# First gate pair: eight loaded operands are split ahead of the first product, four others one step sooner

## The chip, the cores and the metric

The kernel runs on one core of a Trainium2 chip. The metric is the time of one execution on the device in microseconds (us), the median of several runs. Beside it stands one execution taken by the hardware profiler. Its span, from the first instruction to the last, is what the profile divides up; the execution's own time is a little longer. The engines are named PE (matrix products; PEld is its weight load), ACT (ScalarE), DVE (VectorE), POOL (GpSimd) and SP, which here only issues transfers.

## What is computed

One layer of a hybrid encoder over 1024 prompt frames and 32 sample frames (together 1056 columns), model width 1024. The part that matters here is the merge of the two mixers:

```python
h = rms_norm(x, g_mix)
z = h @ w_in                          # q, k, v, conv_h, conv_B, conv_C, gate_a, gate_b
a = attn_core(q, k, v) @ w_attn_out
bo = (cb * conv) @ w_conv_out
x = x + (sigmoid(ga) * a + sigmoid(gb) * bo) @ w_mix_out
```

Ahead of it stand the norm, the input projection and the windowed attention; behind it a cross-attention into 256 memory tokens, a squared-ReLU MLP of width 4096 and a last norm. `ga` and `gb` are two column blocks of `z`, each 1056 columns of frames by 1024 features.

## The kernel before, in words

**Layout and products.** Features lie on the 128 partitions, frames along the columns, in three chunks of 384, 384 and 288 columns (`CH`). Every float32 operand of a product is split into a rounded part `hi` and a remainder `lo`: ACT copies `hi`, DVE subtracts to get `lo`. A product then takes three matmuls per 128 x 128 block: `wh*hi`, `wh*lo`, `wl*hi`. `gemm` (L195) does this over eight blocks, `product` (L875) over the four blocks of half a weight tile.

**Weights.** They stream in tiles of 128 x 1024 (512 KB). `fetch_w` (L147) issues the load on SP into one of two `wr` buffers, or, during the gate pairs, every third one into a further buffer in the pool `gtop`. `issue_w` (L164) splits the oldest loaded tile (L129 on ACT, L130 on DVE) into one of three `wh` and three `wl` buffers. A `wh` buffer is taken again only when the last product that reads it is done.

**The gate pairs.** For each feature block f from 1 to 7, `gate_pair` (L924) computes gate a and gate b of the first two chunks together, with seven half products in place of eight. Weights `w1` (gate a), `w4`, `w3` (sums of gate weights, made beforehand by POOL in `sum_step`, L718) and `w2` (gate b) are used in that order. The operands come in seven kinds, four blocks each: `b11`, `b21`, `t2` and `n1` are split already and lie in `X` tiles; `n3` and `b22` go into `Y` tiles of the middle chunk and `n4` into `N` tiles. These last three kinds were written to memory as plain float32 (`xs_d`) while the attention output was computed, and have to be loaded again and split. In the order of the code a pair is:

- `A = w1 x b11` (L956), copy `s1 <- A` (L958), then one weight split
- `A += w1 x b21` (L962), its sigmoid (L931) and its multiply by the attention output (L935)
- the gate of the 288-column tail with `w1` (`gate_c2`, L966), where it wasn't made earlier: in the pairs 1, 5, 6 and 7
- one weight split, `B = w4 x t2` (L973), `u2 = B - s1` (L976)
- `C = w3 x n1` (L981), `v = C + s1` (L983), `B += w3 x n3` (L984), `B - v` and its sigmoid
- `C += w4 x b22` (L990), `C - u2` (L992) and its multiply by the attention output
- one weight split, `B += w2 x n4` (L997), `B - s1` (L999) and its sigmoid
- one weight split, the tail's gate with `w2` (L1004)

Three times in a pair `sum_step` is called: POOL sends off a load, does four additions of 128 x 256 (L735) on the tile loaded before, and stores it.

**Loading and splitting operands.** `pump(n)` (L807) does two things: it splits everything that the call before has loaded (L810 on ACT, L811 on DVE), and it issues the next n loads of the list `wanted` (L815 on SP). `open_gates` (L884) puts 20 loads on that list: four of `n3`, four of `b22`, four of `n4` and eight of the convolution branch (`bc_d`). It calls `pump(8)` at once, so that `n3` and `b22` are on their way when the first pair begins. The tiles that the first twelve are loaded into are `Gb0` and `Gb1`, five slots each, two of each kind going to `Gb0` and two to `Gb1`. In the first pair `pump(4)` stands behind the sigmoid and multiply of A (L964): it splits the eight and loads the four of `n4`; `pump(0)` at L988, behind product `n3`, splits those four. In the other pairs there are one load at L964 and one at L979.

**What sets the order.** The code gives the order in which instructions are traced. A planner, which runs when the program is built, puts each engine's instructions in an order of its own by a simulated time; within that order each engine then works strictly one after the other, and waits by semaphores. `pin` (L97) holds an instruction behind the one traced just before it on its engine. The splits of `pump` are pinned in this way; its loads are not, and neither are weight splits, the copy to `s1`, or the matmuls.

Of the kernel before, what the change touches and what calls it, by code (L numbers as in the profile page):

```python
# [40 lines left out]
def hybrid_step(ctx: ExitStack, tc: tile.TileContext, io):  # L41
# [5 lines left out]
    def nm(s):  # L47
        uid[0] += 1
        return f"{s}_{uid[0]}"
# [47 lines left out]
    def pin(ins):  # L97
        return tc.keep_in_program_order(ins)

    def acc_tile(shape):  # L100
        return ps.tile(shape, F32, tag="acc", bufs=n_acc, name=nm("acc"))
# [3 lines left out]
    def tmp(n, dt=F32):  # L105
        return tp.tile([P, n], dt, tag="ct", bufs=NCT, name=nm("ct"))
# [40 lines left out]
    def fetch_w(raw=None):  # L147
        if raw is not None:
            pass
        elif third:  # L150
            third["n"] += 1
        if raw is not None:
            pass
        elif third and third["n"] % 3 == 0:
            raw = third["pool"].tile([P, 4, 256], F32, tag="ws", name=nm("wr3")).rearrange("p q c -> p (q c)")
        else:
            raw = wp.tile([P, 1024], F32, tag="wr", bufs=2, name=nm("wr"))
        src = weight(worder[wpos[0] + len(fetched)])
        load = sp.dma_start(raw.rearrange("p (i c) -> p i c", i=4) if len(src.shape) == 3 else raw, src)
        if third and third["n"] == 3 and third["pool"] is W["pool"]:  # L160
            pin(load)
        fetched.append(raw)

    def issue_w(pieces=(slice(0, 1024),)):  # L164
        if not fetched:
            fetch_w()
        raw = fetched.pop(0)
        key = worder[wpos[0]]
        hi = wp.tile([P, 1024], F32R, tag="wh", name=nm("wh"))
        lo = wp.tile([P, 1024], F32R, tag="wl", name=nm("wl"))  # L170
        if kept.get(key) is not None:
            sp.dma_start(lo.bitcast(F32), kept[key])
            act.copy(hi, raw)
        else:
            for at in pieces:
                split(hi[:, at], lo[:, at], raw[:, at])
            if key in kept:
                kept[key] = dram.tile([P, 1024], F32, name=nm("wl_d"))
                sp.dma_start(kept[key], lo.bitcast(F32))
        ready.append((worder[wpos[0]], (hi, lo)))  # L180
        wpos[0] += 1
# [487 lines left out]
    def gate_slot(c, f):  # L669
        n = CH[c][1]  # L670
        return slot(ga_pool, f"Ga{c}", n, F32) if f < 3 else slot(G["pool"], f"Gb{c}", n, F32)
# [46 lines left out]
    def sum_step():  # L718
        old = W.pop("new", None)
        if pieces:  # L720
            at = pieces.pop(0)
            t = sum_tile(len(pieces))
            if at[0] in ("g", "u"):
                kind, f, q = at
                for e in range(2):
                    src = io["w_in"][34 + 8 * e + f] if kind == "g" else io["w_up"][UP[f][e]]
                    src = src.rearrange("p (h c) -> p h c", h=2)
                    pin(pool_e.dma_start(t[:, 2 * e : 2 * e + 2], src[:, :, 256 * q : 256 * q + 256]))
            else:
                pin(pool_e.dma_start(t, io["w_down"][at]))  # L730
            W["new"] = at, t
        if old:
            at, t = old
            for to, x, y in ((3, 2, 3), (2, 0, 2), (0, 0, 3), (1, 1, 0)):
                pin(pool_e.tensor_tensor(t[:, to], t[:, x], t[:, y], op=ALU.add))  # L735
            if at[0] in ("g", "u"):
                kind, f, q = at
                for w in range(2):
                    pin(pool_e.dma_start((gsum_d[f - 1] if kind == "g" else usum_d[f])[:, w, :, 256 * q : 256 * q + 256], t[:, 2 * w : 2 * w + 2]))
            else:  # L740
                pin(pool_e.dma_start(wsum_d[at], t))
# [65 lines left out]
    def pump(n):  # L807
        for into, at, t, get in coming:
            hi, lo = into[at] = (get(), get())
            pin(act.copy(hi, t))  # L810
            pin(dve.tensor_sub(lo, t, hi.bitcast(F32)))  # L811
        coming.clear()
        for into, at, src, cols, get in wanted[:n]:
            t = cols() if callable(cols) else tmp(cols)
            sp.dma_start(t, src)  # L815
            coming.append((into, at, t, get))
        del wanted[:n]
# [57 lines left out]
    def product(acc, w, half, acts, start):  # L875

        wh, wl = w
        for k, (hi, lo) in enumerate(acts):
            a = slice(512 * half + k * P, 512 * half + k * P + P)
            pe.matmul(acc, wh[:, a], hi, start=(start and k == 0), stop=False, skip_group_check=True)  # L880
            pe.matmul(acc, wh[:, a], lo, start=False, stop=False, skip_group_check=True)  # L881
            pe.matmul(acc, wl[:, a], hi, start=False, stop=(k == 3), skip_group_check=True)  # L882
# [22 lines left out]
    def gate_c2(w):  # L905
        n = CH[2][1]
        a = ps.tile([P, n], F32, tag="pt", bufs=2, name=nm("pa"))
        gemm(a, w, xg[2])
        return a
# [14 lines left out]
    def gate_pair(f):  # L924
        def take(key):
            k, w = ready.pop(0)
            assert k == key, (k, key)
            return w

        def into(t, x):  # L930
            act.activation(t, x, AF.Sigmoid)  # L931
            return t

        def attended(c, t):
            dve.tensor_mul(t, t, la[c])  # L935
            sp.dma_start(m1_d[c][:, f], t)

        la = {}

        def load_a(c):  # L940
            if (c, f) in sa:
                return
            la[c] = tmp(CH[c][1])
            sp.dma_start(la[c], a_d[c][:, f])

        op = lambda kind: [gop[kind, k] for k in range(4)]
        w1 = take(("w_in", 34 + f))
        if f == 1:
            third.update(n=2, pool=Y["top"])
            fetch_w()  # L950
        if f == NF - 1:
            third.clear()
        load_a(0)
        load_a(2)
        A, B, C = (acc_tile([P, 384]) for _ in range(3))
        product(A, w1, 0, op("b11"), True)  # L956
        s1 = Y["top"].tile([P, 384], F32, tag="s1", name=nm("s1"))
        act.copy(s1, A)  # L958
        issue_w()
        if f < NF - 1:  # L960
            fetch_w()
        product(A, w1, 1, op("b21"), False)  # L962
        attended(0, into(tmp(384), A))
        pump(4 if f == 1 else 1)  # L964
        if (2, f) not in sa:
            a2 = gate_c2(w1)  # L966
            t = tmp(CH[2][1])
            dve.tensor_mul(t, a2, R[2])
            attended(2, into(t, t))
        issue_w()  # L970
        fetch_w()
        w4 = take(("g_sum", f - 1, 0))
        product(B, w4, 0, op("t2"), True)  # L973
        load_a(1)
        u2 = Y["top"].tile([P, 384], F32, tag="u2", name=nm("u2"))
        dve.tensor_sub(u2, B, s1)  # L976
        sum_step()
        if f > 1:
            pump(1)  # L979
        w3 = take(("g_sum", f - 1, 1))  # L980
        product(C, w3, 1, op("n1"), True)  # L981
        v = Y["top"].tile([P, 384], F32, tag="v", name=nm("v"))
        dve.tensor_add(v, C, s1)  # L983
        product(B, w3, 0, op("n3"), False)  # L984
        g22 = gate_slot(1, f)
        dve.tensor_sub(g22, B, v)
        sg[1][f] = into(g22, g22)
        pump(0)  # L988
        sum_step()
        product(C, w4, 1, op("b22"), False)  # L990
        t = tmp(384)
        dve.tensor_sub(t, C, u2)  # L992
        attended(1, into(t, t))
        issue_w()
        fetch_w()
        w2 = take(("w_in", 42 + f))
        product(B, w2, 1, op("n4"), False)  # L997
        g21 = gate_slot(0, f)
        dve.tensor_sub(g21, B, s1)  # L999
        sg[0][f] = into(g21, g21)  # L1000
        sum_step()
        issue_w()
        fetch_w()
        a2 = gate_c2(w2)  # L1004
        g2 = gate_slot(2, f)
        dve.tensor_mul(g2, a2, R[2])
        sg[2][f] = into(g2, g2)
# [18 lines left out]
    for f in PAIRS:  # L1026
        worder.extend([("w_in", 34 + f), ("g_sum", f - 1, 0), ("g_sum", f - 1, 1), ("w_in", 42 + f)])
        item(lambda f=f: gate_pair(f))
# [992 lines left out]
```

## Time and profile before

| | before |
|---|---|
| runs, median (lowest to highest) | 1748.65 us (1747.12 to 1750.77), 3 runs |
| profiled execution, its own time | 1748.9 us |
| its span | 1746.4 us |
| granted TensorE clock | 0.998 of full speed |
| DMA | 346.60 MB, mean 198 GB/s |
| the seven gate pairs | about 657 to 800 us of the span |

How to read the lines that follow further down. In the page's first part an engine's busy time stands with its share of the span and its number of instructions. A row of the timeline has start, duration, engine, line of the code, operation, output<-inputs, the number of merged instructions, and in brackets the idle time before it with what released it. Numbers at the end of tile names are left out, so that `acc` stands for the accumulators A, B and C alike, `pa` for the tail's gate, `s` for s1, `u` for u2, and `wr` for a raw weight tile wherever it lies. A row of waits has who waited for whom, total, count and longest. A row of stretches has the stretch, its length, then the busy time of PE, PEld, DVE, ACT and POOL with their counts, the granted clock, the share of DMA and GB/s. Rows of SP are marked SPq.

### The profile page before, as it was taken

The page shows a single profiled execution, that of the slowest core. Times are in us where ns is not written, and L with a number is a line of the kernel's source. Part 1 is how long each engine was busy: PE and PEld are TensorE (multiplying, and loading weights), DVE is VectorE, ACT ScalarE, POOL GpSimd, SP SyncE. Part 2 cuts the span into 40 slices and gives each one's busy share as a digit, 9 for nine tenths or more (in the row PEclk, how much of TensorE's full clock was granted, in tenths as well). Part 3 has the DMA queues.
Part 4 walks back from the last instruction along what each step waited for, and adds up shares of the span by engine and source line. Part 5 has one row for each costly group of instructions (what it writes and reads, how often), then busy time and mean ns, then how long its engine had stood idle before and what let it go on. Part 6 is the DMA issues. An engine that isn't in the chain of part 4 may idle for free. (4 is left out here: it accounts for less than half of the span.)

```text
span 1746.4 us, 32603 instructions
## 1 busy us (share of the span) xinstructions
PE 1725.4 (99%) x12262; PEld 1708.0 (98%) x12262; DVE 1192.7 (68%) x2276; ACT 852.7 (49%) x1660; POOL 593.6 (34%) x667
## 2 busy tenths in 40 slices
PE   9999999999999999999999999999999999999998
PEld 8999999999999999999999999999999999999998
DVE  7776776867676656545677888787666686545675
ACT  8653533535335324434556666765444453333444
POOL 0026366453643444452225232005555410000121
PEclk9999999999999999999999999999999999999999
DMA  4333344333436888877766667775767695555555
GB/s 185 99 129 125 119 133 145 121 134 134 156 127 209 288 294 274 281 231 232 270 222 199 217 225 242 234 258 191 222 223 222 217 321 187 189 192 171 191 170 160
DMA packets 179854, 346.60 MB, mean 198 GB/s; under 512 B 18657, under 2 KB 101249, under 8 KB 179569
## 3 DMA queue, kind: packets, MB, share of 16 engines
q1 hardware_dynamic: 163504, 290.07, 50.5%
q0 software_dynamic: 15568, 53.68, 8.8%
q8 instruction: 96, 1.57, 0.4%
q10 hardware_dynamic: 624, 0.77, 0.1%
q14 instruction: 62, 0.50, 0.1%
HBM read 250.73 MB, written 93.14 MB: 197 GB/s over the span
## 5 line engine op out<-in xcount | busy, mean ns | idle before, releaser
L129 ACT CAST wh<-wr 128x1024 fp32r<-128x1024 f32 (+1 forms) x214 | 223.8, 1046 | 369.3 <-PE acc L1808 124.7
L130 DVE TENSOR_TENSOR wl<-wr,wh 128x1024 fp32r<-128x1024 f32 (+1 forms) x214 | 276.4, 1292 | 126.9 <-ACT wh L129 126.2
L200 PE MATMUL acc<-X,wh 128*128 128x384 f32 (+1 forms) x864 | 281.5, 326 | 0.0
L201 PE MATMUL acc<-X,wh 128*128 128x384 f32 (+1 forms) x864 | 278.6, 322 | 0.2 <-DVE X L280 0.2
L202 PE MATMUL acc<-X,wl 128*128 128x384 f32 (+1 forms) x864 | 277.8, 322 | 0.0
L276 POOL TENSOR_TENSOR xacc<-xacc,ct 128x384 f32<-128x384 f32 (+1 forms) x56 | 76.6, 1370 | 379.5 <-ACT ct L274 377.8
L201 PEld LDWEIGHTS acc<-X,wh 128*128 128x128 f32 x864 | 162.7, 188 | 1.5 <-DVE X L280 0.5
L200 PEld LDWEIGHTS acc<-X,wh 128*128 128x128 f32 x864 | 162.4, 188 | 0.9
L202 PEld LDWEIGHTS acc<-X,wl 128*128 128x128 f32 x864 | 162.4, 188 | 0.1
L200 PE MATMUL acc<-Y,wh 128*128 128x384 f32 (+1 forms) x432 | 139.4, 325 | 4.0 <-DVE ct L1066 2.9
L202 PE MATMUL acc<-Y,wl 128*128 128x384 f32 (+1 forms) x432 | 139.2, 323 | 1.8 <-DMA wl<-wl_d 1.8
L201 PE MATMUL acc<-Y,wh 128*128 128x384 f32 (+1 forms) x432 | 139.1, 323 | 0.0
L129 ACT CAST PTh<-pt 128x512 fp32r<-128x512 f32 (+3 forms) x94 | 45.8, 517 | 112.9 <-PE pt L598 111.6
L1807 PE MATMUL acc<-n,wh 128*128 128x264 f32 x352 | 100.2, 285 | 0.0
L1809 PE MATMUL acc<-n,wl 128*128 128x264 f32 x352 | 100.0, 285 | 0.2 <-DVE wl L130 0.2
L1808 PE MATMUL acc<-n,wh 128*128 128x264 f32 x352 | 100.1, 284 | 0.0
L735 POOL TENSOR_TENSOR ws<-ws 128x256 f32<-128x256 f32 x100 | 90.9, 909 | 5.6
L735 POOL TENSOR_TENSOR xacc<-xacc 128x256 f32<-128x256 f32 x100 | 88.9, 889 | 5.7 <-DMA xacc<-in_w_in 0.4
L200 PEld LDWEIGHTS acc<-Y,wh 128*128 128x128 f32 x432 | 80.8, 188 | 5.5 <-DVE ct L1066 3.8
L202 PEld LDWEIGHTS acc<-Y,wl 128*128 128x128 f32 x432 | 81.1, 188 | 2.2 <-DMA wl<-wl_d 2.2
L201 PEld LDWEIGHTS acc<-Y,wh 128*128 128x128 f32 x432 | 81.1, 188 | 0.1
L584 ACT ACTIVATE S<-S,nmx 128x257 f32<-128x257 f32 (+1 forms) x132 | 64.2, 488 | 18.9 <-DVE nmx L579 17.6
(432 smaller groups left out, 5553.7 us busy)
## 6 DMA issues: line engine op xcount, KB each, us to landing
wr<-in_w_up SPq DMA_DIRECT2D x53, 512.0 KB, 4.4
wr<-in_w_in SPq DMA_DIRECT2D x52, 512.0 KB, 3.6
wr<-wsum_d SPq DMA_DIRECT2D x40, 512.0 KB, 3.6
wr<-in_w_conv_out SPq DMA_DIRECT2D x24, 512.0 KB, 3.9
wr<-in_w_mix SPq DMA_DIRECT2D x24, 512.0 KB, 5.0
wr<-in_w_down SPq DMA_DIRECT2D x24, 512.0 KB, 4.1
n_d<-Z SPq DMA_DIRECT2D x32, 264.0 KB, 4.3
xacc<-in_w_down POOLq DMA_DIRECT2D x16, 512.0 KB, 4.6
```

Of the source, the lines that this page charges most:

```text
L129: act.copy(hi, src)
L130: dve.tensor_sub(lo, src, hi.bitcast(F32))
L200: pe.matmul(out, wh[:, a], hi, start=(k == 0), stop=False)
L201: pe.matmul(out, wh[:, a], lo, start=False, stop=False)
L202: pe.matmul(out, wl[:, a], hi, start=False, stop=(k == len(acts) - 1))
L276: pool_e.tensor_tensor(acc, acc, sq, op=ALU.add)
L584: act.activation(stl[:, h, : nk + 1], stl[:, h, : nk + 1], AF.Exp, scale=-1.0, bias=nmx[:, h : h + 1], accum_out=den[:, h : h + 1],)
L735: pin(pool_e.tensor_tensor(t[:, to], t[:, x], t[:, y], op=ALU.add))
L1807: pe.matmul(a, wh[:, s], hi, start=(t == 0 and k == 0), stop=False, skip_group_check=True)
L1808: pe.matmul(a, wh[:, s], lo, start=False, stop=False, skip_group_check=True)
L1809: pe.matmul(a, wl[:, s], hi, start=False, stop=(t == 1 and k == 7), skip_group_check=True)
```

## The change

`pump(4)` of the first pair moves from behind the multiply of A to the head of the pair, behind the loads of the attention output and ahead of product `b11`. The eight splits of `n3` and `b22` and the loads of `n4` move with it. At its old place the first pair now calls `pump(0)` (`f > 1` is False, that is 0), which splits the four `n4` operands there and loads nothing; the call of `pump(0)` at L988 then finds nothing to do in the first pair. For the other pairs `f > 1` is True, that is 1, as before. No instruction is added or taken away, and no buffer changes its size.

```diff
         load_a(0)
         load_a(2)
+        if f == 1:
+            pump(4)
         A, B, C = (acc_tile([P, 384]) for _ in range(3))
         product(A, w1, 0, op("b11"), True)
         s1 = Y["top"].tile([P, 384], F32, tag="s1", name=nm("s1"))
...
             fetch_w()
         product(A, w1, 1, op("b21"), False)
         attended(0, into(tmp(384), A))
-        pump(4 if f == 1 else 1)
+        pump(f > 1)
         if (2, f) not in sa:
             a2 = gate_c2(w1)
             t = tmp(CH[2][1])
```

## The prediction

> **What bounds the kernel now.** I read the page first, then the stretches around the first gate pair, then who waits for whom there, and last the timeline of each engine.
>
> ```profile
> span 1746.4 us, 32603 instructions
> PE 1725.4 (99%) x12262; PEld 1708.0 (98%) x12262; DVE 1192.7 (68%) x2276; ACT 852.7 (49%) x1660; POOL 593.6 (34%) x667
> ```
>
> TensorE sets the time: 1725.4 of 1746.4 us are busy, so no change of order can win more than the 21 us left, and only what lies where the edit acts. The next view gives, for stretches of the first gate pair and the start of the second, the length and then each engine's busy time.
>
> ```profile
> 657.00:671.00 14.00, 14.00 (x92) 14.00 (x91) 6.75 (x8) 7.00 (x14) 8.84 (x11) 1.00 0.84 275
> 671.00:686.00 15.00, 13.22 (x74) 11.97 (x73) 13.90 (x21) 6.75 (x12) 5.89 (x7) 1.00 0.73 253
> 686.00:700.00 14.00, 14.00 (x88) 14.00 (x87) 9.57 (x14) 6.26 (x9) 6.96 (x9) 1.00 0.80 274
> ```
>
> PE is full before 671 and after 686; it loses 15.00 - 13.22 = 1.78 us between. There VectorE is nearly full (13.90 of 15), while in the 14 us before it was busy 6.75. The waits of PE between 640 and 810 us, which holds all seven gate pairs, are these three:
>
> ```profile
> PE acc L880 <- ACT wh L129: 1.0, 1, 1.0
> PE acc L882 <- DVE wl L130: 0.6, 1, 0.6
> PE acc L880 <- ACT s L958: 0.2, 1, 0.2
> ```
>
> A matmul row is longer than the distance to the next one's start, so small losses hide in the overlap. I therefore count starts.
>
> ```profile
> 662.61 0.34 PE L880 MATMUL acc<-X,wh 128*128 128x384 f32 x1
> ...
> 667.16 0.33 PE L882 MATMUL acc<-X,wl 128*128 128x384 f32 x1
> ...
> 668.89 0.29 PE L200 MATMUL pa<-X,wh 128*128 128x288 f32 x1
> ...
> 671.30 0.34 PE L880 MATMUL acc<-Y,wh 128*128 128x384 f32 x1
> ...
> 679.79 0.34 PE L880 MATMUL acc<-N,wh 128*128 128x384 f32 x1
> 680.73 0.44 PE L882 MATMUL acc<-X,wl 128*128 128x384 f32 x1 [0.60 <-DVE wl L130]
> ...
> 683.50 0.34 PE L882 MATMUL acc<-N,wl 128*128 128x384 f32 x1
> 684.84 0.44 PE L880 MATMUL acc<-X,wh 128*128 128x384 f32 x1 [1.00 <-ACT wh L129]
> 685.11 0.34 PE L881 MATMUL acc<-X,wh 128*128 128x384 f32 x1
> 685.63 0.44 PE L880 MATMUL acc<-X,wh 128*128 128x384 f32 x1 [0.18 <-ACT s L958]
> ```
>
> Undisturbed, starts of 384 columns lie about 0.175 us apart (662.61 to 667.16 holds 26 steps). The three breaks lose 0.94 - 0.18 = 0.76, 1.34 - 0.18 = 1.16 and 0.52 - 0.18 = 0.34 us. Beside the breaks single starts are late too, as that of 685.11, 0.27 behind its forerunner; five such make 0.5. Together 2.75 us, the most that the edit can take away where it acts. [...]
>
> **Why PE waits there.** ACT first, then DVE, POOL and SP.
>
> ```profile
> 657.54 0.40 ACT L829 COPY ct<-acc 128x288 f32<-128x288 f32 x1 [2.69 <-PE acc L202]
> 659.61 0.48 ACT L958 COPY s<-acc 128x384 f32<-128x384 f32 x1 [1.66 <-PE acc L882]
> 661.31 1.05 ACT L129 CAST wh<-wr 128x1024 fp32r<-128x1024 f32 x1 [1.23 <-DMA wr<-gsum_d]
> ...
> 665.71 0.48 ACT L931 ACTIVATE ct<-acc 128x384 f32<-128x384 f32 x1
> ...
> 666.84 2.98 ACT L810 CAST Y<-Gb 128x384 fp32r<-128x384 f32 x7
> ...
> 683.74 1.04 ACT L129 CAST wh<-wr 128x1024 fp32r<-128x1024 f32 x1 [4.71 <-issue]
> ```
>
> ```profile
> 662.40 1.23 DVE L130 TENSOR_TENSOR wl<-wr,wh 128x1024 fp32r<-128x1024 f32 x1 [13.89 <-ACT wh L129]
> ...
> 665.84 2.13 DVE L130 TENSOR_TENSOR wl<-wr,wh 128x1024 fp32r<-128x1024 f32 x1 [1.85 <-ACT wh L129]
> 667.89 1.09 DVE L935 TENSOR_TENSOR ct<-ct,ct 128x384 f32<-128x384 f32 x1
> 668.90 1.09 DVE L811 TENSOR_TENSOR Y<-Gb,Y 128x384 fp32r<-128x384 f32 x1
> 669.92 0.55 DVE L976 TENSOR_TENSOR u<-acc,s 128x384 f32<-128x384 f32 x1
> ...
> 670.84 1.48 DVE L811 TENSOR_TENSOR Y<-Gb,Y 128x384 fp32r<-128x384 f32 x3
> ...
> 677.48 1.51 DVE L811 TENSOR_TENSOR N<-Gb,N 128x384 fp32r<-128x384 f32 x1
> 678.92 1.75 DVE L130 TENSOR_TENSOR wl<-wr,wh 128x1024 fp32r<-128x1024 f32 x1
> ...
> 682.61 0.55 DVE L811 TENSOR_TENSOR N<-Gb,N 128x384 fp32r<-128x384 f32 x1
> ```
>
> ```profile
> 657.98 3.21 POOL L735 TENSOR_TENSOR xacc<-xacc 128x256 f32<-128x256 f32 x4
> ...
> 666.12 4.47 POOL L735 TENSOR_TENSOR ws<-ws 128x256 f32<-128x256 f32 x4
> ```
>
> ```profile
> 645.85 2.31 SPq L815 DMA_DIRECT2D Gb<-xs_n  x2
> ...
> 667.99 0.32 SPq L159 DMA_DIRECT2D wr<-gsum_d  x1
> ...
> 671.41 0.32 SPq L815 DMA_DIRECT2D Gb<-xs_n  x1
> ```
>
> VectorE sits idle for 13.89 us up to 662.40, then meets weights, eight splits (L811 into Y) and four more (into N) at once. The last N split ends at 683.16, the product that reads it (n4) at 683.84. Its weight buffer is one of three, so the cast at 683.74, of the second pair's third weight, had to wait for it (I read "issue" there as that release, since its load left SP at 667.99). The cast's end, 684.78, releases PE. That is the 1.16. The 0.76 is the weight split that starts at 678.92, right behind a 1.51 us N split.
>
> **The change part by part.** Durations are those rows'.
>
> *Eight splits earlier.* Eight ACT casts at 2.98/7 = 0.43 us and eight DVE subtractions at 1.48/3 = 0.49 move, none is added. Pinned now behind the last attention-output copy, they start at 657.94, when their slots (read by the middle chunk's product) and their loads are long done. ACT is through 3.4 us later, at 661.4. The copy of s1 may slip from 659.61 behind them and ends by 661.9 at worst; the second half of A needs it at 662.61, and the tail-chunk gate product runs on PE until then. So 0, and with that cover gone up to 661.9 - 659.4 = 2.5 us. The cast of 661.31 slips to 661.9 at most, which its half-word split passes on.
>
> On DVE the eight begin at 658.4, beside POOL's four adds. Rows: an add alone takes 3.21/4 = 0.80 and beside DVE 4.47/4 = 1.12; a subtraction 0.49 alone and 1.09 beside POOL. Four at 1.09 and four at 0.49 end at 664.7, the weight split behind them (1.23) at 666.0; the third matmul of n1 reads it at 667.16, so 1.2 us remain. Were all eight at 1.09 and that split at 2.13 (its slowest row), it would end at 669.2, 2.1 late. I take 0, nearest to the rows of that very stretch. Below nothing: these eight no longer delay the split of 665.84, but PE did not wait on it.
>
> [...]
>
> *The n4 loads.* Two of four already left at 645.85; the other two need slots that the first splits free, and move (the later one from 671.41) to about 660, ahead of two weight loads and an attention load on SP. SP's issue is 0.32 us each, and it idles there, waiting for weight splits. They share the DMA engines with the weight that lands at 661.3; 0.39 MB at the stretch's 275 GB/s is 1.4 us, which at worst makes its split end at 667.4, 0.2 late. I take 0.
>
> *Four splits a step sooner.* Their ACT part (1.7 us) follows the sigmoid of 665.71 and ends by about 668; their DVE part follows the multiply L935, from 669.0: two at 1.09 until POOL's adds end at 670.59, two at 0.49, done at 672.1. Behind them on DVE may wait u2 (669.92 now, then up to 672.1, ending 672.7), and product n3 accumulates where u2 reads. PE has 24 matmuls of the other tail-chunk gate (from 668.89, 24 x 0.134 = 3.2 us; 18 of them fill 668.89 to 671.30) to fill up to 672.1. So between 0 (u2 goes first) and 0.6; without the filler 672.7 - 668.9 = 3.8. I take 0: in the rows u2 overtook the three Y splits of 670.84, which the code has ahead of it.
>
> *What goes.* N is ready at 672, well before the n4 matmul of 679.79. The weight split of 678.92 starts when its cast ends, 677.8, and even at 1.75 ends at 679.5, against 679.97 needed: 0.76 + 0.10 gone. n4 can then run in one piece and release its buffer near 679 to 680; the cast of 683.74 moves up by some 4 us and 1.16 + 0.30 go. The third (0.34 + 0.10) is the second pair's s1, queued behind that cast; it may go or be met again since that pair has no tail product to cover it: I leave it in. Sum: 2.75 - 0.44 = 2.3 us. Next late would be the same weights in pair 2, where PE has no gap today.
>
> **Total.** The profiled execution took 1748.9 us, 2.5 beyond its span; the three runs have a median of 1748.65 (1747.12 to 1750.77). Own time: 1748.9 - 2.3 = 1746.6; on the median: 1746.4 (rounded up from 1746.35). A measurement of this kernel can tell about 0.2%, 3.5 us, from no change, so I forecast no change that shows, of negative sign.
>
> **Rivals.**
>
> - *The forecast* (chance 0.52): 1745.5 to 1748.
> - *The wait moves to u2* (0.13), the slower side. Place: DVE after 669. It decides if u2 ends after PE is through n1 and what it has been given as filler. The planner fixes PE's order beforehand; if it sets n3 straight behind n1 at 668.9, PE stands 3.8 us. With the 2.3 gone that is +1.5, 1750.2; if the weights then are late as now, +3.8, 1752.5. Against: PE has the filler in today's order. For: today it was called on because the Y splits were late, which they no longer are.
> [...]
> - *The planner deals later work anew.* The order is planned for the whole program, and a shift here may change who is first at 870 to 1190 us, where PE loses most of what remains:
>
> ```profile
> PE acc L200 <- DVE ct L1066: 2.9, 3, 1.4
> PE acc L202 <- DMA wl<-wl_d: 1.8, 1, 1.8
> ```
>
>  By starts, all losses behind 810 us sum to 15 us, half of it small. If these two rows' 4.7 go in part (1.5 to 3), the time is 1743.4 to 1744.9 (0.18); if about 6 us of such waits come in, 1752.4 (0.07).
> - *It doesn't do what it says* (0.05): the planner puts weights and s1 first and the splits stay near 666: 1748.65.
>
> Faster by over 0.2% (below 1745.15) is the first planner case, 0.18; slower (above 1752.15) the second, 0.07, and the bad end of u2, 0.05: 0.12; within, 0.70. The range 1743.6 to 1751.0 leaves out the far end of the good planner case (0.04) and those above (0.14).
>
> **What would show it.** Right: L810 and L811 into Y between 658 and 665, into N between 666 and 673; the cast of 683.74 near 679; PE busy some 15 of 15 in the stretch now at 13.22; the three waits reduced to L958 at most. Wrong: n3's first matmul waiting for DVE u; n1 waiting for a weight split at 667; s1 holding the second half of A; or a span that moves by other than that stretch's gain, with the waits behind 810 us changed.

## The result and the profile after

| | before | changed |
|---|---|---|
| runs, median (lowest to highest) | 1750.68 us (1746.73 to 1755.36), 22 runs | 1747.66 us (1743.34 to 1750.64), 22 runs |
| ratio | | 0.9983, 95% interval 0.9977 to 0.9990 |
| profiled execution, its own time | 1748.9 us | 1749.59 us |
| its span, mean granted clock | 1746.4 us, 0.998 | 1747.8 us, 0.995 |

The change wins 3.0 us, with an interval of 1.75 to 4.0; 2.3 were forecast. The two profiled executions say the opposite, 1.4 us longer by their spans and 0.7 by their own times, and the first thing to learn here is why. Of the profile after, the head of the page comes first, then the stretches with the columns as before, and two short ones for the granted clock (the third number from the end).

```profile
span 1747.8 us, 32606 instructions
PE 1727.7 (99%) x12262; PEld 1712.4 (98%) x12262; DVE 1188.1 (68%) x2276; ACT 852.9 (49%) x1660; POOL 586.2 (34%) x667
```

```profile
657.00:671.00 14.00, 12.13 (x77) 11.90 (x76) 9.80 (x15) 7.58 (x16) 5.33 (x6) 0.98 0.81 289
671.00:686.00 15.00, 15.00 (x83) 15.00 (x83) 9.06 (x14) 5.39 (x8) 9.10 (x12) 0.91 0.82 257
686.00:700.00 14.00, 14.00 (x89) 14.00 (x88) 9.67 (x13) 6.82 (x11) 5.62 (x7) 1.00 0.83 293
670.00:672.00 2.00, 2.00 (x12) 2.00 (x11) 2.00 (x5) 0.14 (x1) 0.43 (x1) 0.60 0.56 131
672.00:674.00 2.00, 2.00 (x9) 2.00 (x9) 1.16 (x3) 0.00 (x0) 1.90 (x3) 0.55 1.03 325
```

The stretch of 671 to 686, which had 13.22 us of PE, is full, and VectorE's 13.90 there are down to 9.06, as meant. But the stretch ahead of it has lost 1.87, and then comes something that before's trace does not show in this place: from 670.4 to 673.8 the granted clock is a half. PE counts as busy all the while, only slower: 15.00 busy with 83 matmuls in place of 90 or so. The wait, and the matmuls behind it:

```profile
PE pa L202 <- DVE wl L130: 1.9, 1, 1.9
```

```profile
667.41 0.29 PE L201 MATMUL pa<-X,wh 128*128 128x288 f32 x1
669.57 0.40 PE L202 MATMUL pa<-X,wl 128*128 128x288 f32 x1 [1.87 <-DVE wl L130]
...
670.20 0.29 PE L200 MATMUL pa<-X,wh 128*128 128x288 f32 x1
...
670.75 0.44 PE L200 MATMUL pa<-X,wh 128*128 128x288 f32 x1
670.99 0.44 PE L201 MATMUL pa<-X,wh 128*128 128x288 f32 x1
```

The three waits of before are gone, all three. In their place PE waits once, in the tail's gate with `w2`, for the remainder of the fourth weight tile; 1.2 us behind it starts lie 0.24 us apart (670.75 to 670.99) where 0.13 is usual. Counted by starts the changed kernel loses 3.52 us between 630 and 810 in this execution, 2.03 in the wait and 1.5 at the halved clock behind it; before loses 2.75. What delayed that remainder is on ACT, then DVE, then SP and POOL:

```profile
656.23 1.34 ACT L810 CAST Y<-Gb 128x384 fp32r<-128x384 f32 x3
658.00 0.48 ACT L960 COPY s<-acc 128x384 f32<-128x384 f32 x1 [0.43 <-PE acc L882]
658.37 0.52 ACT L810 CAST Y<-Gb 128x384 fp32r<-128x384 f32 x1
661.94 1.05 ACT L129 CAST wh<-wr 128x1024 fp32r<-128x1024 f32 x1 [3.06 <-DMA wr<-gsum_d]
662.90 1.75 ACT L810 CAST Y<-Gb 128x384 fp32r<-128x384 f32 x4
664.55 1.05 ACT L129 CAST wh<-wr 128x1024 fp32r<-128x1024 f32 x1
...
665.88 0.50 ACT L810 CAST N<-Gb 128x384 fp32r<-128x384 f32 x1
...
668.82 1.33 ACT L810 CAST N<-Gb 128x384 fp32r<-128x384 f32 x3
```

```profile
663.03 1.48 DVE L130 TENSOR_TENSOR wl<-wr,wh 128x1024 fp32r<-128x1024 f32 x1 [3.55 <-ACT wh L129]
664.43 3.59 DVE L811 TENSOR_TENSOR Y<-Gb,Y 128x384 fp32r<-128x384 f32 x4
667.94 0.44 DVE L970 TENSOR_TENSOR ct<-pa,R 128x288 f32<-128x288 f32 x1
668.31 1.21 DVE L130 TENSOR_TENSOR wl<-wr,wh 128x1024 fp32r<-128x1024 f32 x1
...
670.38 0.55 DVE L978 TENSOR_TENSOR u<-acc,s 128x384 f32<-128x384 f32 x1
```

```profile
655.75 0.32 SPq L159 DMA_DIRECT2D wr<-gsum_d  x1
```

```profile
662.66 4.47 POOL L735 TENSOR_TENSOR ws<-ws 128x256 f32<-128x256 f32 x4
```

The eight splits do not run in one piece. The planner has put the cast of a weight (L129 at 661.94, here the third weight) between the fourth and the fifth, and the second four stand behind it on ACT, as on DVE. That weight left SP at 655.75 and landed only at 661.9, 6.2 us later; before, 657.36 to 661.3. So ACT stands idle for 3.06 us with four casts behind it whose operands have long been loaded. The second four then run at 3.59 / 4 = 0.90 us beside POOL's additions in place of 0.49, and the fourth weight's split, behind them, comes too late. Two causes are thus in the profile, a late landing (theory B) and the additions (theory A). That the new wait and the halved clock happen in this execution, and how often, is what the runs had to say.

### The profile page after: what moved, and what is told of

The parts are those of the page before. It is cut to its first block, busy times and chain, and to the rows that moved or that the text cites. A ratio compares the mean times of both kernels' runs of the same rounds, so it can differ in the third digit from the quotient of the medians.

```text
span 1747.8 us, 32606 instructions
## 1 busy us (share of the span) xinstructions
PE 1727.7 (99%) x12262; PEld 1712.4 (98%) x12262; DVE 1188.1 (68%) x2276; ACT 852.9 (49%) x1660; POOL 586.2 (34%) x667
## 5 line engine op out<-in xcount | busy, mean ns | idle before, releaser
L129 ACT CAST wh<-wr 128x1024 fp32r<-128x1024 f32 (+1 forms) x214 | 223.8, 1046 | 366.6 <-PE acc L1810 121.4
L129 ACT CAST PTh<-pt 128x512 fp32r<-128x512 f32 (+3 forms) x94 | 45.8, 516 | 112.8 <-PE pt L598 111.4
```

Source lines behind the costliest of these rows:

```text
L129: act.copy(hi, src)
```

## The experiments

All medians are beside runs of before on the same chip. "Lost" is counted by starts between 630 and 810 us in the one profiled execution of each, a halved clock there included.

| kernel | median us (runs) | before us (runs) | ratio, 95% interval | lost, us |
|---|---|---|---|---|
| changed, first | 1747.66 (22) | 1750.68 (22) | 0.9983 (0.9977 to 0.9990) | 3.52 |
| e1, before again | 1750.44 (12) | 1748.82 (35) | 1.0006 (0.9994 to 1.0018) | 2.43 |
| e2, changed again | 1748.42 (12) | 1748.82 (35) | 1.0002 (0.9988 to 1.0015) | 0.00 |
| e3, eight alone | 1750.10 (12) | 1748.82 (35) | 1.0001 (0.9989 to 1.0014) | 2.32 |
| e4, four alone | 1749.51 (12) | 1748.82 (35) | 1.0005 (0.9994 to 1.0015) | 0.92 |
| e5, changed, third time | 1747.39 (12) | 1749.63 (29) | 0.9983 (0.9971 to 0.9996) | 0.51 |
| e6, changed, third weight earlier | 1747.55 (12) | 1749.63 (29) | 0.9988 (0.9976 to 1.0000) | 0.00 |
| e7, third weight earlier alone | 1750.49 (12) | 1749.63 (29) | 1.0005 (0.9992 to 1.0018) | 1.69 |
| e8, changed, six sums left out | 1748.39 (10) | 1750.50 (25) | 0.9982 (0.9969 to 0.9996) | 1.31 |
| e9, changed, additions twice | 1751.49 (10) | 1750.50 (25) | 1.0009 (0.9997 to 1.0021) | 1.42 |
| e10, e9 with the third weight earlier | 1748.57 (10) | 1750.50 (25) | 0.9987 (0.9976 to 0.9997) | 0.00 |
| e11, four alone again | 1749.79 (12) | 1748.84 (23) | 1.0003 (0.9992 to 1.0014) | 3.59 |
| e12, changed, fourth time | 1749.07 (12) | 1748.84 (23) | 0.9996 (0.9982 to 1.0010) | 0.00 |

**Both kernels again (e1, e2, e5, e12).** No edit.

> The kernel before, unchanged, against itself. Both theories: ratio 1.000 within 0.0012. Its profiled execution shows how much one execution differs from another: the theory that the stretch of the first pair sets the difference expects again 2 to 3.5 us lost between 655 and 690 us, by the same three waits (weight split, cast behind n4, copy of s1). The rival, that executions differ mostly by short stretches of halved TensorE clock that follow long waits, expects the same waits but a mean clock that moves between 0.994 and 0.998 and the time with it, about 1.7 us for each 0.001.

> The changed kernel, with its lines numbered as before. Ratio near 0.9983. Theory 1 (the gain is the lost time of the first pair, and the new wait of PE for the lower half of the fourth weight comes only when the third weight lands late): the cast of the third weight before 660.5 us, counted from a span that reaches the pair at 657, and no wait of PE for L130, so 0 to 1 us lost in the stretch; if that weight lands over 5 us after its issue, the wait of about 2 us again. Theory 2 (the wait belongs to the new order itself): PE waits for L130 by 1.5 to 2 us however early the third weight lands, and the gain must come from elsewhere, such as fewer stretches of halved clock.

> The changed kernel a third time, to compare with the two that follow on the same chip and for one more profiled execution. The theory that the landing of the third weight decides: if it lands within 4.5 us of its issue, PE loses under 0.5 us in the stretch of the first pair, if it takes over 5.5 us, PE waits about 2 us for the lower half of the fourth weight. The rival, that what decides is when POOL's additions fall on the eight splits: a wait whenever four splits take over 3 us, whatever the landing. Time: 1 to 3 us under the kernel before.

> The full change, a third time beside before on one chip. Expected 2.0 to 3.0 us under before (ratio 0.9983 to 0.9989), span times clock about 1738.2. If its earlier gain was a matter of the chip or of the halved clock, it lies within 0.7 us of before. In the profile, the fourth weight's remainder (L130) ends between 666 and 669.5 us, by when the third weight landed; PE waits for it only where that landing was later than about 661 us.

The stretches of e2, whose pair begins 0.9 us sooner than before's, taken 2 us earlier, and those of e12:

```profile
655.00:669.00 14.00, 14.00 (x92) 14.00 (x91) 11.54 (x16) 8.65 (x18) 6.65 (x9) 1.00 0.83 273
669.00:684.00 15.00, 15.00 (x92) 15.00 (x91) 10.83 (x13) 5.27 (x8) 8.58 (x10) 1.00 0.79 277
```

```profile
657.00:671.00 14.00, 14.00 (x92) 14.00 (x91) 12.21 (x19) 8.54 (x18) 5.81 (x7) 1.00 0.83 279
671.00:686.00 15.00, 15.00 (x90) 15.00 (x89) 7.76 (x9) 5.52 (x9) 8.54 (x12) 1.00 0.82 278
```

Nothing is lost there, in either. What is different in e2 is the same part of ACT and of DVE:

```profile
660.49 1.05 ACT L129 CAST wh<-wr 128x1024 fp32r<-128x1024 f32 x1 [0.91 <-DMA wr<-gsum_d]
661.45 1.75 ACT L810 CAST Y<-Gb 128x384 fp32r<-128x384 f32 x4
```

```profile
662.76 1.95 DVE L811 TENSOR_TENSOR Y<-Gb,Y 128x384 fp32r<-128x384 f32 x4
664.64 0.44 DVE L968 TENSOR_TENSOR ct<-pa,R 128x288 f32<-128x288 f32 x1
665.01 1.21 DVE L130 TENSOR_TENSOR wl<-wr,wh 128x1024 fp32r<-128x1024 f32 x1
```

The weight landed in 4.0 us, POOL's additions fell at 657.5 and 667.5 and not on the second four, and the fourth weight's remainder was ready at 666.2, 2 us ahead of its use. e12 shows that the additions alone do not make the wait. They do fall on its second four, but its weight had landed in 3.8 us, and the fourth weight's remainder is ready at 667.3, 1.1 us ahead of its use:

```profile
659.94 4.47 POOL L735 TENSOR_TENSOR ws<-ws 128x256 f32<-128x256 f32 x4
```

```profile
662.72 3.04 DVE L811 TENSOR_TENSOR Y<-Gb,Y 128x384 fp32r<-128x384 f32 x4
```

In e5 the weight took 5.4 us, the second four ran alone in 1.96 and the additions fell on the fourth weight's split instead: 0.51 lost by starts, no wait. So the profile that comes with a result is one execution; of four of the changed kernel two lost nothing here, one 0.51 and one 3.52. Before varies too: e1 has no wait for the weight split (0.76 by starts in the first profile, 0.28 here) and loses 2.43 in place of 2.75. In time the four sessions disagree as well: two show the gain, two (e2, e12) cannot tell it from none, and e12 by itself stayed within the 0.7 us that its expectation gave to the rival. The differences of the means are -3.3, -0.2, -2.9 and -0.7 us; weighted by their scatter, -2.2 with 95% limits of about -3.0 and -1.4. A second measure takes the clock out: the span times its mean granted clock, averaged over the runs, is 1738.6 us for the 58 runs of the changed kernel and 1740.5 for the 112 of before beside e1 to e12, 2.0 less. The first session has no such figure for before, though. Where both have it, on one chip, the changed kernel is 1.2 (e2), 2.3 (e5) and 1.2 (e12) less, together 1.6 with 95% limits of 1.0 and 2.2. I hold 1.6 to 2.2 for the better size of the gain, and the 3.0 of the first session for its upper part.

**One part of the change alone (e3, e4, e11).** e3 is the change with nothing called at L964 in the first pair, so that the four stay at L988; e4 and e11 leave the eight where they were and split the four one `pump` earlier.

```diff
 # e3
+        f == 1 and pump(4)
...
-        pump(4 if f == 1 else 1)
+        f > 1 and pump(1)
 # e4 and e11, ahead of w3
-        if f > 1:
-            pump(1)
+        pump(f > 1)
```

> Only the eight splits go ahead of the first product; the four of n4 are split where they were, behind product n3. Theory 1, as the prediction has it: the eight take away most of what crowds VectorE after 665, so the N splits run undisturbed at about 675 to 677 and the three waits shrink from 2.75 us to under 1; ratio 0.9985 to 0.9990. Rival: the step of the four is what frees the weight buffer early; then the cast behind n4 stays late and the ratio is 0.9995 to 1.000.

> Only the four n4 operands are split one step sooner, at the place ahead of product n3, while the eight stay behind the multiply of A. Theory 1: VectorE stays crowded from 665 to 680, since nothing used its idle time before, so the waits stay between 1.5 and 3 us; ratio 0.9995 to 1.0005. Rival (the step of the four frees the buffer): the cast behind n4 comes 3 to 4 us earlier and the ratio is 0.9988 or lower.

> The four splits alone once more, beside the full change on the same chip. In its first profile this kernel had lost only 0.92 us by starts between 630 and 810 us, against 2.75 for before, but its time did not show it. If what is lost by starts in that stretch is the time, the median lies 1.5 to 2 us under before, near 1748, two thirds or more of what the full change wins. If the gain of the full change comes from elsewhere, or the eight are needed for it, the median lies within 0.7 us of before while the full change stays 2 or more under it. For both the span times its granted clock is the sharper measure (expected 1738.5 to 1739 by the first, 1740 to 1740.6 by the second).

Neither part wins; the gain that e3 was expected to show (a ratio of 0.9985 to 0.9990) did not come. In e3 the old wait for the cast of the second pair's weight is there in full, because the four N splits still come late; its waits of PE between 640 and 810 and ACT's rows:

```profile
PE acc L880 <- ACT wh L129: 1.0, 1, 1.0
PE acc L880 <- ACT s L958: 0.2, 1, 0.2
```

```profile
676.34 0.50 ACT L810 CAST N<-Gb 128x384 fp32r<-128x384 f32 x1
676.74 0.44 ACT L931 ACTIVATE Ga<-Ga 128x288 f32<-128x288 f32 x1
681.62 1.04 ACT L129 CAST wh<-wr 128x1024 fp32r<-128x1024 f32 x1 [4.44 <-issue]
```

In e4 the loss by starts fell to 0.92, as if the four were the whole change, but its time did not follow. A second execution of the same kernel, e11, shows what the four need (SP's loads, ACT, then PE):

```profile
670.18 0.61 SPq L815 DMA_DIRECT2D Gb<-xs_n  x1
671.86 0.48 SPq L815 DMA_DIRECT2D Gb<-xs_n  x1
```

```profile
664.57 2.00 ACT L129 CAST wh<-wr 128x1024 fp32r<-128x1024 f32 x2 [5.82 <-DMA wr<-gsum_d]
...
676.06 0.51 ACT L810 CAST N<-Gb 128x384 fp32r<-128x384 f32 x1 [4.64 <-DMA Gb<-xs_n]
676.98 0.51 ACT L810 CAST N<-Gb 128x384 fp32r<-128x384 f32 x1 [0.41 <-DMA Gb<-xs_n]
677.40 1.04 ACT L129 CAST wh<-wr 128x1024 fp32r<-128x1024 f32 x1
```

```profile
678.49 0.45 PE L880 MATMUL acc<-X,wh 128*128 128x384 f32 x1 [1.99 <-ACT wh L129]
```

Two of the four `n4` loads need the slots of the eight. With the eight at their old place they leave at 670.18 and 671.86 and land at 676.0 and 677.0; the casts of N, now ahead in ACT's order, wait for them, and the weight cast of the second pair stands behind. In e4 the same two casts wait 2.39 and 1.80 us. Of the 3.59 us that e11 loses by starts 2.15 are this wait; another 1.2 or so, near 666, come of the third weight, whose load took 8.4 us there (first row of ACT) and which stands ahead of the four in ACT's order. So each part needs the other: the eight free the slots, the four use them. Over e4 and e11 the four alone are at +0.6 us (95% limits -0.4 and +1.6), where 1.8 less had followed from e4's profile. The sessions' own changed kernels do not settle this alone: e12, beside e11, was only 0.7 us under before in the means.

**The new wait (e6, e7).** The counter by which every third fetch gets the further buffer (`fetch_w`) begins at another place, so that buffers change hands among the weights: the load of the third weight leaves at 648.45 us in e6, not at 656.44 as in e2.

```diff
-            third.update(n=2, pool=Y["top"])
+            third.update(n=0, pool=Y["top"])
```

> The changed kernel, with the rotation of the extra weight buffer shifted by two, so that the third weight of the first pair goes into a buffer that is free some 10 us earlier; the order of PE stays the same. If its late landing is what can bring the new wait, its cast now comes before 654 us, nothing holds up the second four of the eight splits, they end by 662 and PE loses nothing in the stretch, in whichever execution; time 1747 or lower, at least as good as the changed kernel. The rival (additions of POOL): up to 2 us lost all the same. The second weight of the next pair now waits for the late buffer; if that is worse, a wait shows near 677 to 685.

> The kernel before with that shift of the buffer alone. Both theories: the waits behind n4 stay (2 to 2.75 us lost between 676 and 686), since the splits stay where they were; ratio 0.9995 to 1.0005.

e6 has no wait and no loss: that weight is cast at 657.97, ahead of the eight, and among the eight only the copy to s1 comes between. POOL's additions did not fall on the eight in this execution, so e6 says nothing of them. In time it is not to be told from the changed kernel beside it (1747.55 and 1747.39). Without the change the same edit wins nothing (e7).

**Landing or additions (e8, e9, e10).** `sum_step`'s loop of four additions is run no times (e8, shown) or twice (e9, a 2 in place of the 0) for six tiles around the first pair; e10 is e9 with the edit of e6.

```diff
-            at, t = old
-            for to, x, y in ((3, 2, 3), (2, 0, 2), (0, 0, 3), (1, 1, 0)):
+            at, t, W["k"] = *old, W.get("k", -1) + 1
+            for to, x, y in ((3, 2, 3), (2, 0, 2), (0, 0, 3), (1, 1, 0)) * (0 if 36 <= W["k"] <= 41 else 1):
```

> The changed kernel without the additions of POOL for the six weight tiles that it handles around the first pair; these six sums are left out. PE's order is that of the changed kernel. Theory A (the wait of the changed kernel's first profile, 1.87 us for the lower half of the fourth weight, came of additions beside the second four of the eight splits): the eight take 0.49 us each in both groups, each weight split 1.23, and PE waits under 0.3 us for L130 in the stretch, even if the third weight lands late. Theory B (the late landing alone): a landing over 5.5 us after the issue brings 1 us or more again.

> The changed kernel with the additions of those six tiles done twice over, so that these sums are wrong; the orders of PE, ACT and DVE are those of the changed kernel. Theory A: POOL's additions now take 7 to 9 us of each tile and nearly always lie beside the splits; two groups of four take 3.6 to 4.4 us each, the split of the fourth weight ends 1.5 to 3 us later, and PE waits 1 to 3 us for L130 before the middle of the pair; time 1 to 4 us over the changed kernel, more if a stretch of halved clock follows. Theory B: a wait only where the third weight lands over 5.5 us after its issue.

> The additions twice over, as in the run before (six sums wrong), and the third weight early, as in the run with the shifted buffer. Theory A: the eight splits run from about 660 in one piece at up to 1.09 us each, so the eight end near 668 and the fourth weight's split is late all the same, PE waits 0.5 to 3 us. Theory B: with the landing out of the way no wait over 0.3 us.

e8, ACT, then DVE, then PE:

```profile
663.70 1.05 ACT L129 CAST wh<-wr 128x1024 fp32r<-128x1024 f32 x1 [4.14 <-DMA wr<-gsum_d]
```

```profile
665.92 1.96 DVE L811 TENSOR_TENSOR Y<-Gb,Y 128x384 fp32r<-128x384 f32 x4
```

```profile
669.43 0.40 PE L202 MATMUL pa<-X,wl 128*128 128x288 f32 x1 [1.06 <-DVE wl L130]
```

With not one addition in sight the four take 1.96, as they do alone, and PE still waits 1.06 us, since the weight took 7.3 us (656.42 to 663.70). That is theory B by itself. e9 is theory A: the weight took 4.7 us (656.98 to 661.64), but the second four stand beside doubled additions:

```profile
663.86 4.14 DVE L811 TENSOR_TENSOR Y<-Gb,Y 128x384 fp32r<-128x384 f32 x4
```

```profile
663.30 8.99 POOL L735 TENSOR_TENSOR xacc<-xacc 128x256 f32<-128x256 f32 x8
```

```profile
669.73 0.40 PE L202 MATMUL pa<-X,wl 128*128 128x288 f32 x1 [0.80 <-DVE wl L130]
```

4.14 - 1.96 = 2.2 us more, for a wait of 0.80. So neither theory holds alone: a landing of 7.3 us makes the wait without additions, and doubled additions make it at a landing of 4.7; additions as they are did not at 3.8 (e12). In the first profile both had a part, the additions with 3.59 - 1.96 = 1.6 of its 1.87 us. What both need is the order: four splits behind a weight that may be late, and another weight behind the four. e10 takes that order away and leaves the doubled additions. They end at 662.4 and so lie beside the first four of the eight, as many as in e9:

```profile
658.67 6.01 DVE L811 TENSOR_TENSOR Y<-Gb,Y 128x384 fp32r<-128x384 f32 x8
```

The eight end at 664.7, and there is no wait and no loss at all; what e10 was expected to show by theory A (a wait of 0.5 to 3 us) did not come. e9 and e10 differ in the code by the edit of e6 alone. In time they differ by 2.9 us in their medians and 1.8 in their means, with 95% limits of about -0.1 and 3.7, so that it is the profiles that tell them apart.

## Why the prediction was right, and where it was not

The time (1747.66 for 1746.4, within its range), the sign, and the size (2.3 for 3.0 in the first session, 1.6 to 2.2 over four) came out, and by the mechanism given. That the time lies so near is in part luck: the base was 2.0 us too low (1748.65 from three runs, 1750.68 from 22), and the 0.7 more that the first session won made up for some of it. And "no change that shows" rested on telling 0.2% apart; 22 runs on either side told 0.17%. By its steps:

- *What goes*, 2.3 of 2.75: right, though its first term, 0.76, is not a constant of the kernel (0.28 in e1). In e2 and e12 all of the 2.75 is gone, the 0.44 of s1 too, which I had left in. "The cast of 683.74 moves up by some 4 us": counted from the first matmul of the pair, the second pair's third cast starts at 26.4 in before and 25.9 in e1, at 21.2 in e2 and e12, so 4.8 to 5.3 sooner.
- *u2 goes first* and costs 0: right. In the profile after it starts at 670.38, behind one N split and ahead of three. The rival in which PE waits for u2 falls.
- *The copy of s1* was expected behind the eight, up to 661.9; the planner put it ahead of the fourth (658.00). No cost either way.
- *Eight splits earlier, cost 0*: right in most executions, wrong in its picture. I had all eight ahead of the weight cast and a margin of 1.2 us at the third matmul of n1. The planner put that cast between the fourth and the fifth, and the step then hangs on when the weight lands; what is late next is the fourth weight, in the tail's gate, which the prediction does not name. It costs 0 in e2 and e12, 0.5 in e5 and a wait of 1.87 us in the first profile, within the 2.1 that I had kept as a bound, for a partly different reason; the 1.5 us of halved clock behind that wait had no place in the sum.
- *The n4 loads, 0*: the cost is right as far as the runs show, since the landing of the weight (3.8 us in e12, 7.3 in e8) scatters more than the 1.4 us that I feared. But they leave at 658.6, behind the weight and not ahead of it; and their worth was missed: I counted them as a cost alone, while e11 shows them to be what the four splits wait for.
- *Four splits a step sooner, 0 to 0.6, taken 0*: right, with the eight moved. The sum credited "what goes" to the four without saying that they need the eight. The two single edits are what shows it.
- *Subtractions at 1.09 us beside POOL's additions, 0.49 alone*: slower beside them as taken, on average by less. Four took 3.59 us in the first profile after, 0.90 each, and 1.95 in e2 with no addition beside them. In e9, beside the doubled additions, they took 4.14, 1.04 each; in that time POOL, at 1.12 us an addition (8.99 us for eight), did 3.7. My estimate from the rows for each alone, one after the other, is 4 x 0.49 + 3.7 x 0.80 = 4.9 us, 0.8 more than measured.
- *The planner deals later work anew*: it does not. Set side by side, before and e2 differ in the order of PE, ACT, DVE and SP between 660 and 715 us alone, that is in the first pair and the start of the second; POOL's order is the same. The waits at 870 scatter from run to run (1.84 in before, 2.31 in e2, 2.68 in the first profile after) in an order that did not change.
- *Own time of the profiled execution as the base*: the sum gave 1746.6 for an execution that took 1749.59. Counted by the start of the same matmul in both profiles, the changed kernel reaches the pair 1.6 us sooner, loses 0.8 us on before within it, where it was to win 2.3, and loses 2.4 more near 870, where a longer wait and a halved clock behind it stand. So the sum failed for this execution in the pair itself, by the new wait and the halved clock behind it; by the same count e2, e6, e10 and e12 win 2.9 us in the pair and e5 2.4.

What stays open: why the weight's load takes 3.8 us in one execution of the changed kernel (e12) and 6.2 in another, 7.3 in e8 and 8.4 in e11. POOL's loads and stores lie up to 6 us apart between executions and may hold it up, but no run held their phase fixed, so this is not shown.

## What to carry to other kernels

When work is moved into idle time, ask what the planned order of each engine will place between its pieces: a piece behind an operand that is still in flight makes everything behind it late too (ACT stood idle for 3.06 us in the first profile after, with four loaded casts behind that piece), and what took the wait away here was to have that operand sooner (e6, e10), though e6's median is no better than the changed kernel's. Two moves that each win nothing may be one change: a load freed by the one is what the other waits for. And where a change is worth 0.1%, one profiled execution can show it with the wrong sign; take the order from the profile, and the size from many runs, with the clock taken out.

## What the runs showed of the hardware

**Halved clock.** In its one execution before's trace shows full clock but for its last 7 us; e1, the same kernel, has four stretches at a granted clock of 0.5 (from 997, 1048, 1079 and 1140 us). The changed kernel has three in its first profile (670, 872, 1138), each 3.41 us long, and in e2 one from 868.3, where matmuls of 384 columns start 0.32 us apart for 0.17. By these figures 3.41 us at half the clock cost some 1.7 us. With the clock taken out, as above, the standard deviation of before's 112 runs falls from 2.6 to 1.6 us, so that most of the scatter between runs goes with the clock; a line through these runs gives about 2.0 us for 0.001 of the mean clock. Three slow stretches that follow one long wait of PE stand behind waits of 1.87 (the first profile after, 669.57), 2.31 (e2, 867.83) and 2.68 us (the first profile after, 871.22); before's wait of 1.84 at 871.19 had none behind it.

Length alone does not sort these waits: e11's 1.99 us at 678.49 had none either. The stretches near 1046 (e11, e12) and the one at 1138 (the first profile after) follow no wait of PE over 0.50 us in the 10 us ahead of them. What brings a slow stretch no run here shows.
